# The high and low parts of each streamed weight, issued at the scheduler's highest priority

## The chip, the cores and the metric

The kernel runs on one core of one Trainium2 chip. The metric is device time in microseconds (us), the median of several executions. The core has five engines with one instruction stream each: PE (matrix multiply, with its weight loads listed apart as PEld), DVE (vector), ACT (scalar), POOL and SP, which here only starts DMAs. Each engine runs its own stream strictly in order.

## The reference, cut to what matters

The model has two layers over 256 latent tokens and 256 context tokens, width 1024. Each layer is

```python
h = h + 0.5 * gate * swiglu(modulate(rms_norm(h)), w_up1, w_down1)
u = modulate(rms_norm(h)) @ w_in          # one wide projection
a = [gqa(u), hyena(u), neighbourhood(u), mla(u)]   # four mixers side by side
m = sum_b sigmoid(u_gate[b]) * (a[b] @ w_branch[b])
h = h + gate * (m @ w_out)
h = h + 0.5 * gate * swiglu(modulate(rms_norm(h)), w_up2, w_down2)
```

followed by a last RMS norm of the 256 latent tokens. Everything is float32. All the weights are read once.

## The kernel before, in words

**Three products for one.** A float32 operand x is split into a high part (x rounded to the type fp32r) and a low part (the rest). `split` (L222 to 225) does that with two instructions: a CAST on ACT (L224) writes the high part, a subtraction on DVE (L225) writes the low part and needs the high part first. `mm3` (L246 to 252) then multiplies high by high (L250), high by low (L251) and low by high (L252) into one PSUM bank.

**Weights.** `load` (L227 to 243) brings one block of weights: a tile `raw` in three buffers, filled by one DMA on SP's queue (L235), and the tiles `whi` and `wlo`, most of them in two buffers each. A block of more than 1024 columns is split in two halves, so that each load gives two CASTs and two subtractions. There are 268 loads, 536 halves. In the rows, a CAST of L224 that writes `whi` and a subtraction of L225 that writes `wlo` are these. Other calls of `split` write activations: `ph`/`pl` (feed-forward), `pth`/`ptl` (transposed attention probabilities), `nV`, `gV`, `o`, `mo` and so on; they have the same two lines.

**Stages.** Feed-forward stages stream `up` and `dn` weights through PE. Between them stand a norm (`norm_pair`, output `nh`/`nl`) and the mixers. A mixer works head by head: `head_a` makes the scores `s` (L721), adds a bias in the neighbourhood mixer (L723, from `bm`), takes the negative maximum `nm` (L724), the exponential `P` on ACT (L725), the reciprocal `rs` (L737), and scales `P` on POOL (L740). `head_b` transposes `P` on PE into `ptb` (L755 and L760), splits it into `pth`/`ptl`, and multiplies with the values into `ob` (L767). `of` (L769, L770) collects the heads. In the neighbourhood mixer each head also needs four small DMAs `braw` (L945) on SP's queue, into one buffer, and two POOL additions that make `bm` of it (L948).

**What fills PE beside the heads.** The gates and branch projections (`merge_list`, weights `wmg`, one load a column block: L1085 `th`, L1089, and `merged` on POOL, L1090) are cut in units and dealt out between the heads, so that PE has matmuls `mmb` while a head's chain runs on ACT, DVE and POOL. Layer 0 works on 512 tokens, layer 1 after its first feed-forward on 256, where a matmul is half as wide and there is less to fill with.

**What sets the order.** The kernel is written for a tile framework. It takes the instructions in program order as a rank, lets each engine's next instruction be the one of best rank among those that its model of the chip holds for ready, and writes the five streams out; the streams are then fixed, and on the chip an instruction that waits holds up everything behind it on its engine. `tc.high_priority()` raises whatever is issued inside it above the rest of the kernel.

Of the kernel before, what the change touches and what calls it, by code (L numbers as in the profile page):

```python
# [185 lines left out]
class Net:  # L186
# [40 lines left out]
    def load(self, src, shape, pool=None, bufs=2):  # L227
        nc = self.nc
        n = int(np.prod(shape))
        raw = self.wp.tile([128, 2048], F32, tag="raw", name="raw", bufs=3)  # L230
        hi = (pool or self.wp).tile([128, 2048], F32R, tag="whi", name="whi", bufs=bufs)
        lo = (pool or self.wp).tile([128, 2048], F32R, tag="wlo", name="wlo", bufs=bufs)
        nd = len(shape)
        pat = "p " + " ".join("abcd"[:nd]) + " -> p (" + " ".join("abcd"[:nd]) + ")"
        nc.sync.dma_start(out=raw[:, :n], in_=src.rearrange(pat) if nd > 1 else src)  # L235
        parts = 1 if n <= 1024 else 2
        step = n // parts
        for s in range(0, n, step):
            self.split(hi[:, s:s + step], lo[:, s:s + step], raw[:, s:s + step])
        kw = {"abcd"[i]: shape[i] for i in range(nd)}  # L240
        back = "p (" + " ".join("abcd"[:nd]) + ") -> p " + " ".join("abcd"[:nd])
        if nd == 1:
            return hi[:, :n], lo[:, :n]
        return hi[:, :n].rearrange(back, **kw), lo[:, :n].rearrange(back, **kw)
# [206 lines left out]
    def ffn_lead(self, l, which, n):  # L451
        up = self.a[f"up{which}"][l]

        def lead(load):
            ws = [load(i, up[i], [2, 8, 128]) for i in range(2)]
            ps = [[], []]

            def step(f, k0, a, b):
                if not ps[f]:
                    ps[f] += [self.sbank(), self.bank()] if f else [self.bank(), self.sbank()]  # L460
                for k in range(k0, k0 + 4):
                    for i in range(2):
                        self.mm3(ps[f][i][:, a:b], [(ws[f][0][:, i, k], ws[f][1][:, i, k], self.nh[:, k, a:b], self.nl[:, k, a:b])],
                                 k == 0, k == KT - 1)

            return [lambda f=f, k=k, a=a, b=b: step(f, k, a, b) for g, a, b in self.groups(n) for f in range(2) for k in (0, 4)], ps
        return lead

    def mla_lead(self, l):
        def lead(load):  # L470
            ws = [load(i, self.a["wmkv"][l, i], [4, 288]) for i in range(2)]
            out = []

            def step(g, half):
                if half == 0:
                    out.extend((2 * g + i, (self.sbank() if i else self.bank())[:, 0:288]) for i in range(2))
                wh, wl = ws[half]
                for k in range(4):
                    for tt, p in out[-2:]:
                        s = slice(128 * tt, 128 * tt + 128)  # L480
                        self.mm3(p, [(self.nh[:, 4 * half + k, s], self.nl[:, 4 * half + k, s], wh[:, k, :], wl[:, k, :])],
                                 half == 0 and k == 0, half == 1 and k == 3)

            return [lambda g=g, half=half: step(g, half) for g in range(2) for half in range(2)], out
        return lead
# [826 lines left out]
```

## Time and profile before

| | |
|---|---|
| median of 3 executions | 2529.19 us (2528.36 to 2530.41) |
| profiled execution | 2528.62 us |
| its span | 2526.7 us (1.92 us lie outside it) |
| PE busy | 2444.3 us, 97% of the span |
| DVE, ACT, POOL busy | 1566.2, 1036.5, 322.2 us |
| mean granted TensorE clock | 0.994 of full speed |

A row of the trace names the line, the engine, the operation and the tiles (out <- in, buffer numbers left out). "Idle before" is time in which that engine did nothing ahead of the instruction, with the instruction or DMA that ended it. PE is idle for 82 us in all, which is what an order of instructions could win at most.

### The profile page before, as it was taken

What the parts mean: (1) busy time and instruction counts of PE and PEld (TensorE: products, weight loads), DVE (VectorE), ACT (ScalarE), POOL (GpSimd) and SP (SyncE); (2) the same over time, 40 slices, a digit from 0 to 9 for tenths busy, and PEclk for the clock granted to TensorE, in tenths of its full rate; (3) what the DMA queues carried; (4) which work ended last, traced back from release to release, by engine and by line L of the source; (5) the groups of instructions that cost most, each with busy time, mean ns of one, the idle gap of its engine ahead of it and who ended that gap; (6) DMA issues with size and microseconds to landing.
All of it is one profiled execution on the core that took longest, in us unless ns stands there. A gap on an engine that the chain in (4) does not pass through costs nothing.

```text
span 2526.7 us, 34201 instructions
## 1 busy us (share of the span) xinstructions
PE 2444.3 (97%) x13452; PEld 2089.5 (83%) x13452; DVE 1566.2 (62%) x2520; ACT 1036.5 (41%) x1813; POOL 322.2 (13%) x378
## 2 busy tenths in 40 slices
PE   6999999999989999999999999999999999999998
PEld 3788888877878788788888888888888898798998
DVE  5779865477466555657795355543357767676555
ACT  3422223466236444433222243222246646555443
POOL 3100001111113132211000010000021112221000
PEclk9999999999999999999999999999999999999999
DMA  7556544132212344334563244552232433555453
GB/s 270 209 184 222 202 157 150 57 104 85 95 51 75 72 102 92 121 117 150 184 231 144 84 141 179 174 188 95 76 115 99 143 124 104 104 138 180 153 207 109
DMA packets 80632, 346.74 MB, mean 137 GB/s; under 512 B 24726, under 2 KB 30552, under 8 KB 54360
## 3 DMA queue, kind: packets, MB, share of 16 engines
q1 hardware_dynamic: 78744, 341.41, 40.6%
q10 hardware_dynamic: 1728, 3.15, 0.3%
q8 instruction: 106, 1.74, 0.3%
q14 instruction: 54, 0.44, 0.1%
HBM read 333.52 MB, written 6.82 MB: 135 GB/s over the span
## 4 chain that ended last, share of the span: by engine, by line
PE 77%; issue 10%; DVE 5%; POOL 3%; ACT 3%; DMA 2%; SPq 0%; POOLq 0%; DVEq 0%; ACTq 0%
PE mmb L250 22%; PE mmb L251 22%; PE mmb L252 22%; PE ob L767 2%; PE s L721 1%; DVE wlo L225 1%; DMA braw<-in_rpb 1%; PE ptb L755 1%; POOL P L740 1%; POOL nv L375 1%; ACT whi L224 1%; PE sb L582 1%; PE s L730 1%; PE sb L250 1%; PE sb L252 1%
## 5 line engine op out<-in xcount | busy, mean ns | idle before, releaser
L252 PE MATMUL mmb<-nh,wlo 128*128 128x512 f32 (+1 forms) x2224 | 786.3, 354 | 7.1 <-DVE wlo L225 7.1
L250 PE MATMUL mmb<-nh,whi 128*128 128x512 f32 (+1 forms) x2224 | 787.5, 354 | 3.7 <-ACT nh L374 1.4
L251 PE MATMUL mmb<-nl,whi 128*128 128x512 f32 (+1 forms) x2224 | 785.5, 353 | 3.3 <-DVE nl L376 3.2
L224 ACT CAST whi<-raw 128x1024 fp32r<-128x1024 f32 (+4 forms) x536 | 475.0, 920 | 727.5 <-PE mmb L251 619.6
L225 DVE TENSOR_TENSOR wlo<-raw,whi 128x1024 fp32r<-128x1024 f32 (+4 forms) x536 | 580.8, 1106 | 101.0 <-ACT whi L224 89.0
L252 PEld LDWEIGHTS mmb<-nh,wlo 128*128 128x128 f32 x2224 | 422.0, 190 | 65.0 <-DVE wlo L225 9.5
L251 PEld LDWEIGHTS mmb<-nl,whi 128*128 128x128 f32 x2224 | 422.0, 190 | 61.8 <-DVE nl L376 6.0
L250 PEld LDWEIGHTS mmb<-nh,whi 128*128 128x128 f32 x2224 | 422.5, 190 | 61.1 <-ACT nh L374 2.2
L251 PE MATMUL mmb<-pl,whi 128*128 128x512 f32 (+1 forms) x770 | 267.1, 347 | 0.0
L252 PE MATMUL mmb<-ph,wlo 128*128 128x512 f32 (+1 forms) x770 | 267.1, 347 | 0.0
L250 PE MATMUL mmb<-ph,whi 128*128 128x512 f32 (+1 forms) x770 | 266.8, 347 | 0.0
L430 DVE TENSOR_TENSOR s<-s,mmb 128x512 f32<-128x512 f32 (+1 forms) x85 | 52.7, 620 | 241.1 <-PE mmb L252 233.3
L314 DVE SCALAR_TENSOR_TENSOR vraw<-vraw,cb 128x1024 f32<-128x1024 f32 x128 | 155.5, 1223 | 34.3 <-DMA vraw<-in_adat 27.1
L345 POOL TENSOR_TENSOR rstd<-msq,nhalf 128x2 f32<-128x2 f32 (+1 forms) x11 | 8.4, 765 | 1303.7 <-DVE msq L344 1303.7
L250 PEld LDWEIGHTS mmb<-ph,whi 128*128 128x128 f32 x770 | 145.8, 189 | 18.2
L252 PEld LDWEIGHTS mmb<-ph,wlo 128*128 128x128 f32 x770 | 145.8, 189 | 18.1
L251 PEld LDWEIGHTS mmb<-pl,whi 128*128 128x128 f32 x770 | 145.8, 189 | 17.9
L314 DVE SCALAR_TENSOR_TENSOR scr<-vraw,cb 128x1024 f32<-128x1024 f32 x96 | 117.1, 1220 | 41.3 <-DMA vraw<-in_adat 35.6
L386 DVE SCALAR_TENSOR_TENSOR h<-mmb,mods,h 128x256 f32<-128x256 f32 x136 | 61.2, 479 | 123.9 <-PE mmb L252 123.9
L740 POOL TENSOR_SCALAR P<-P,rs 128x512 f32<-128x512 f32 (+1 forms) x144 | 97.5, 695 | 308.3 <-DVE rs L737 255.3
L429 ACT ACTIVATE s<-mmb 128x512 f32<-128x512 f32 (+1 forms) x85 | 46.4, 546 | 211.2 <-PE mmb L252 211.2
L250 PE MATMUL mmb<-whi,nh 128*128 128x512 f32 (+3 forms) x256 | 89.2, 348 | 2.8 <-ACT nh L374 2.8
(280 smaller groups left out, 3469.0 us busy)
## 6 DMA issues: line engine op xcount, KB each, us to landing
raw<-in_up SPq DMA_DIRECT2D x88, 1024.0 KB, 4.8
vraw<-in_adat SPq DMA_DIRECT2D x64, 1024.0 KB, 4.8
raw<-in_wmg SPq DMA_DIRECT2D x64, 768.0 KB, 4.4
raw<-in_dn SPq DMA_DIRECT2D x64, 704.0 KB, 4.1
raw<-in_wh SPq DMA_DIRECT2D x12, 1024.0 KB, 4.8
araw<-in_adaw SPq DMA_DIRECT2D x8, 1024.0 KB, 9.1
raw<-in_wnqk SPq DMA_DIRECT2D x8, 1024.0 KB, 4.8
raw<-in_wo SPq DMA_DIRECT2D x8, 1024.0 KB, 4.9
```

The lines of the kernel that those rows point to most:

```text
L224: nc.scalar.copy(hi, src)
L225: nc.vector.tensor_tensor(lo, src, hi.bitcast(F32), ALU.subtract)
L250: nc.tensor.matmul(out, wh, xh, start=start and i == 0, stop=False)
L251: nc.tensor.matmul(out, wh, xl, start=False, stop=False)
L252: nc.tensor.matmul(out, wl, xh, start=False, stop=stop and i == n - 1)
L314: nc.vector.scalar_tensor_tensor(out, raw[:, j], 1.0, self.cb[:, s], ALU.mult, ALU.mult, accum_out=mc[:, j, s:s + 1])
L375: nc.gpsimd.tensor_scalar(v[:, i], t[:, i], sc, sh, ALU.mult, ALU.add)
L386: self.nc.vector.scalar_tensor_tensor(h[:, j, a:b], ps[:, a:b], self.mods[l][:, 8 * chunk + j, g:g + 1], h[:, j, a:b], ALU.mult, ALU.add)
L429: nc.scalar.activation(s[:, :n], pa[:, :n], AF.Silu)
L430: nc.vector.tensor_tensor(s[:, :n], s[:, :n], pg[:, :n], ALU.mult)
L740: nc.gpsimd.tensor_scalar(sl, sl, rs[:, qt:qt + 1], 0.0, ALU.mult, ALU.add)
L767: nc.tensor.matmul(ob[:, 0:p.shape[1]], vst(kt), p, start=i + j == 0, stop=i + j == len(pts))
```

## The change

The call of `split` inside `load` is put under `high_priority`. Splits of activations, and those of the Fourier tables that are made elsewhere, keep their rank.

```diff
         for s in range(0, n, step):
-            self.split(hi[:, s:s + step], lo[:, s:s + step], raw[:, s:s + step])
+            with self.tc.high_priority():
+                self.split(hi[:, s:s + step], lo[:, s:s + step], raw[:, s:s + step])
```

No instruction is added or taken away. The same instructions stand in another order: on ACT 146 of the 536 weight CASTs are ahead of something they were behind before (5 are later), on DVE 199 of the subtractions (26 later). The lines below L238 have a number that is one higher in the changed kernel.

**First place: SP's queue in layer 1's neighbourhood mixer.** `raw_18303` is a block of 128x2048 of the query and key weights `wnqk`; `braw` are the bias DMAs of one head each. Before:

```order
L235 DMA raw_18012<-in_wnqk 128x2048
L945 DMA braw_17904<-in_rpb 64x4x64 x4
L235 DMA raw_18115<-in_wmg 128x1536
L945 DMA braw_18088<-in_rpb 64x4x64 x4
L235 DMA raw_18222<-in_wmg 128x1536
L945 DMA braw_18195<-in_rpb 64x4x64 x4
L235 DMA raw_18303<-in_wnqk 128x2048
L235 DMA raw_18406<-in_wmg 128x1536
L945 DMA braw_18379<-in_rpb 64x4x64 x4
```

Now:

```order
L235 DMA raw_18012<-in_wnqk 128x2048
L235 DMA raw_18115<-in_wmg 128x1536
L946 DMA braw_17904<-in_rpb 64x4x64 x4
L235 DMA raw_18222<-in_wmg 128x1536
L946 DMA braw_18088<-in_rpb 64x4x64 x4
L235 DMA raw_18303<-in_wnqk 128x2048
L946 DMA braw_18195<-in_rpb 64x4x64 x4
L235 DMA raw_18406<-in_wmg 128x1536
L235 DMA raw_18513<-in_wmg 128x1536
```

Each weight block has moved ahead of one group of four bias DMAs.

**Second place: ACT in the same stretch.** `pth_18172` and `pth_18181` are the two halves of the transposed probabilities of one head (of `P_17914`, made before these rows), `P_18098` and `P_18205` the exponentials of the next two heads. Before:

```order
L1085 ACTIVATE th_18161<-mmb_18123 128x256
L725 ACTIVATE P_18098,sum_18097<-s_18099,nm_18096 128x512
L725 ACTIVATE P_18098,sum_18097<-s_18105,nm_18096 128x512
L224 CAST whi_18304<-raw_18303 128x1024
L224 CAST pth_18172<-ptb_18167 128x512
L224 CAST pth_18181<-ptb_18176 128x512
L224 CAST whi_18304<-raw_18303 128x1024
L769 COPY of_18165<-ob_18166 64x256
```

Now:

```order
L1086 ACTIVATE th_18161<-mmb_18123 128x256
L224 CAST pth_18172<-ptb_18167 128x512
L726 ACTIVATE P_18098,sum_18097<-s_18099,nm_18096 128x512
L224 CAST whi_18304<-raw_18303 128x1024 x2
L726 ACTIVATE P_18098,sum_18097<-s_18105,nm_18096 128x512
L224 CAST pth_18181<-ptb_18176 128x512
L1086 ACTIVATE th_18268<-mmb_18230 128x256
L770 COPY of_18165<-ob_18166 64x256
```

The first half of `whi_18304` stood ahead of both `pth`; now both of its halves stand behind `pth_18172` and ahead of `pth_18181`.

**Third place: DVE in layer 0's grouped-query mixer (GQA), at a load of `wnv` weights (`wlo_6946`).** `ptl_6663`, `ptl_6672` and `ptl_6681` are the low parts of one head's transposed probabilities. Before:

```order
L1089 SCALAR_TENSOR_TENSOR th_6651<-th_6651,mmb_6614 128x512
L225 TENSOR_TENSOR wlo_6946<-raw_6944,whi_6945 128x1024
L225 TENSOR_TENSOR ptl_6663<-ptb_6657,pth_6662 128x512
L225 TENSOR_TENSOR ptl_6672<-ptb_6666,pth_6671 128x512
L225 TENSOR_TENSOR wlo_6946<-raw_6944,whi_6945 128x1024
L225 TENSOR_TENSOR ptl_6681<-ptb_6675,pth_6680 128x512
```

Now:

```order
L1090 SCALAR_TENSOR_TENSOR th_6651<-th_6651,mmb_6614 128x512
L225 TENSOR_TENSOR wlo_6946<-raw_6944,whi_6945 128x1024 x2
L225 TENSOR_TENSOR ptl_6663<-ptb_6657,pth_6662 128x512
L225 TENSOR_TENSOR ptl_6672<-ptb_6666,pth_6671 128x512
L225 TENSOR_TENSOR ptl_6681<-ptb_6675,pth_6680 128x512
```

The second half of the weight's low part has moved ahead of two low parts of the head. On ACT the second half of `whi_6945` has moved ahead of `pth_6662` and `pth_6671` in the same way.

## Rows read from the trace of the kernel before

**Rows 1.** The page: span, busy time, two groups of instructions.

```profile
span 2526.7 us, 34201 instructions
PE 2444.3 (97%) x13452; PEld 2089.5 (83%) x13452; DVE 1566.2 (62%) x2520; ACT 1036.5 (41%) x1813; POOL 322.2 (13%) x378
...
L224 ACT CAST whi<-raw 128x1024 fp32r<-128x1024 f32 (+4 forms) x536 | 475.0, 920 | 727.5 <-PE mmb L251 619.6
L225 DVE TENSOR_TENSOR wlo<-raw,whi 128x1024 fp32r<-128x1024 f32 (+4 forms) x536 | 580.8, 1106 | 101.0 <-ACT whi L224 89.0
```

**Rows 2.** Busy time by stage (us, instructions); window; last columns clock, DMA share, GB/s.

```profile
100.00:400.00 300.00, 300.00 (x1325) 248.43 (x1324) 235.49 (x394) 82.98 (x111) 0.00 (x0) 1.00 0.54 192
400.00:620.00 220.00, 213.06 (x1166) 181.29 (x1165) 131.65 (x221) 118.20 (x247) 40.41 (x60) 0.99 0.27 85
...
740.00:860.00 120.00, 117.76 (x593) 93.62 (x594) 74.27 (x112) 67.30 (x147) 34.46 (x41) 0.99 0.22 77
...
1925.00:2010.00 85.00, 76.75 (x512) 66.54 (x511) 69.15 (x129) 62.90 (x137) 11.77 (x16) 0.98 0.31 107
...
2140.00:2265.00 125.00, 117.60 (x779) 105.60 (x778) 84.70 (x142) 70.29 (x136) 36.07 (x43) 0.99 0.52 110
```

**Rows 3.** PE's waits over the whole span: us in total, times, longest.

```profile
PE mmb L252 <- DVE wlo L225: 7.1, 6, 3.6
...
PE mmb L250 <- ACT nh L374: 4.2, 3, 1.4
```

**Rows 4.** Timeline of PE, 2204 to 2213 us.

```profile
2204.34 1.04 PE L755 MATMUL ptb<-ident,P 128*128 128x128 f32 x8
2205.14 1.18 PE L721 MATMUL s<-K,Q 128*128 128x512 f32 x4
2211.53 0.58 PE L767 MATMUL ob<-pth,nV 128*128 128x256 f32 x1 [5.21 <-ACT pth L224]
```

**Rows 5.** Timeline of ACT in the same stretch.

```profile
2205.00 0.20 ACT L725 ACTIVATION_READ_ACCUMULATOR P<-s,nm 128x1 f32 x1
2209.94 1.04 ACT L224 CAST whi<-raw 128x1024 fp32r<-128x1024 f32 x1 [4.75 <-DMA raw<-in_wnqk]
2210.89 1.07 ACT L224 CAST pth<-ptb 128x512 fp32r<-128x512 f32 x2
```

**Rows 6.** Timeline of SP's DMA issues, 2168 to 2250 us.

```profile
2184.47 2.57 SPq L945 DMA_DIRECT2D braw<-in_rpb  x4
...
2195.61 2.57 SPq L945 DMA_DIRECT2D braw<-in_rpb  x4
2198.28 0.55 SPq L235 DMA_DIRECT2D raw<-in_wnqk  x1
```

**Rows 7.** Timeline of POOL and DVE, 2184 to 2200 us.

```profile
2185.12 3.69 POOL L740 TENSOR_SCALAR P<-P,rs 128x512 f32<-128x512 f32 x2
...
2195.57 1.36 POOL L740 TENSOR_SCALAR P<-P,rs 128x512 f32<-128x512 f32 x2
...
2187.05 1.20 DVE L225 TENSOR_TENSOR wlo<-raw,whi 128x1024 fp32r<-128x1024 f32 x1
```

**Rows 8.** Timeline of ACT, DVE, PE, POOL, 824 to 831 us.

```profile
825.05 1.05 ACT L224 CAST whi<-raw 128x1024 fp32r<-128x1024 f32 x1 [1.83 <-PE mmb L251]
...
826.12 2.37 DVE L225 TENSOR_TENSOR wlo<-raw,whi 128x1024 fp32r<-128x1024 f32 x1
828.42 1.27 DVE L225 TENSOR_TENSOR ptl<-ptb,pth 128x512 fp32r<-128x512 f32 x2
...
829.15 0.66 PE L755 MATMUL ptb<-ident,P 128*128 128x128 f32 x4 [0.64 <-DVE ptl L225]
...
826.12 1.29 POOL L1090 TENSOR_TENSOR merged<-merged,th 128x512 f32<-128x512 f32 x1 [0.98 <-DVE th L1089]
```

**Rows 9.** Timeline of ACT, 1955 to 1990 us (MLA of layer 1).

```profile
1966.54 0.84 ACT L224 CAST whi<-raw 128x768 fp32r<-128x768 f32 x1 [2.79 <-issue]
...
1969.43 0.84 ACT L224 CAST whi<-raw 128x768 fp32r<-128x768 f32 x1
```

## The prediction, made before the changed kernel ran

> **What bounds the kernel now.** I read the page first: PE is busy for 2444.3 of 2526.7 us [rows 1]. The change makes no instruction shorter, so all it can win lies in the 82.4 us in which PE is idle; what it can lose has no such limit. So the second view is busy time by stage [rows 2]. In the feed-forward stretch from 100 to 400 us PE is busy for 300.00 of 300.00 us: no weight is ever late there, and none can come usefully earlier. The CASTs show why: ACT's idle time before them is 619.6 us for PE, that is, they wait until PE has given back the weight buffer, then run at once, one pair of buffers ahead [rows 1]. PE is idle beside the mixers: 6.9 us from 400 to 620 (MLA of layer 0), 2.2 us from 740 to 860 (GQA of layer 0), 8.3 us from 1925 to 2010 (MLA of layer 1), 7.4 us from 2140 to 2265 (neighbourhood mixer of layer 1) [rows 2].
>
> Third, the list of waits. For a weight's low part, which the change is to bring earlier, PE waits 7.1 us in 6 places, 3.6 us of it in one [rows 3]. The longest of these (at 736 us, behind a normalisation that waits for POOL) and most of the rest have the same neighbours in the new order as in the old, so I count nothing for them. The time that I do count is the other way about: a weight's CAST that holds up an attention head. At 2206.3 us PE has ended the scores `s` and then stands for 5.21 us before `ob` [rows 4], because `pth` is not there. ACT was idle for 4.75 us ahead of a `whi` CAST that waited for its DMA, `raw` of `wnqk`, with `pth` queued right behind it [rows 5].
>
> **The change part by part.**
>
> *No work is added.* 536 CASTs and 536 subtractions (0.920 and 1.106 us each on average [rows 1]) stay what they are. The sum is one of places.
>
> *The neighbourhood mixer of layer 1: −4.6 us.* Two moves bear on the stall. On ACT `pth_18172` now stands ahead of `whi_18304` (second place). Its transposes end at 2205.4 us [rows 4] and the exponentials ahead of it at 2205.2 [rows 5], so it can end near 2206.0, before PE is done with the scores at 2206.3: that wait of 5.21 us goes. The other half, `pth_18181`, stands behind two halves of 1.04 us and an exponential; PE has some 18 matmuls of filling between the two halves in its new order, at 0.12 us about 2.1 us, against 2 x 1.04 + 0.6 = 2.7 us: 0.6 us is left, if the weight has landed. It should have. Before, the DMA was issued at 2198.28 us behind four `braw` that began at 2195.61 [rows 6], and the CAST could start at 2209.94 [rows 5], 11.7 us after the issue. Now it stands ahead of that group, behind the one that began at 2184.47 and took 2.57 us [rows 6]; its buffer comes free when the subtraction that began at 2187.05 ends, at 2188.3 [rows 7]. Issued then, it lands by 2200 even if it takes 11.7 us again, five microseconds before its CAST. So −5.21 + 0.6 = −4.6 us. The bounds: −5.2 if nothing is left, 0 if the wait comes back as another.
>
> *GQA of layer 0: +1.8 us.* Here a weight's second half passes two low parts of a head (third place). Before, the first `wlo` ran from 826.12 for 2.37 us, then two `ptl` for 1.27 together; PE, which needs the `ptl` buffer back before it transposes again, stood for 0.64 us until 829.15 [rows 8]. Now the second `wlo` comes between: 1.20 us [rows 7], so that `ptl_6663` ends near 830.3 instead of 829.1. On ACT `pth_6662` moves back by one CAST, 1.05 us [rows 8]. PE fills some of it: 12 filling matmuls instead of 9 before the next transposes, at 0.227 us each 0.7 us. Net +1.2 − 0.7, about +0.6 us with the rest of the pipeline. There are two such loads (`wnv`). Five or six `wmg` loads among the heads show the same exchange with shorter halves and no stall now; 0.1 us each, together 0.6. Sum 2 x 0.6 + 0.6 = +1.8; bounds 0 (PE finds other filling) and +3.
>
> *MLA of layer 0: +0.5 us.* Weights' halves pass up to ten attention instructions on ACT, and PE takes its filling sooner, so that the late heads have less beside them. PE is idle for 6.9 us in the stretch now [rows 2]. The bounds are 0 and +3, four or five halves of 0.84 us [rows 9] uncovered; as 512-token matmuls still stand between the heads I take a value near the lower end.
>
> *MLA of layer 1: 0.* PE has least to fill with here (8.3 us idle of 85 [rows 2]) and the reorder is largest. At 1966.54 and 1969.43 stand two halves of one load, of 0.84 us each, with five kinds of head work between [rows 9]; now they run next to each other, so that the second half is 2 us earlier and the head work 0.84 us later. PE waited on both sides in this stretch, for weights and for heads. Bounds ±3 us, middle taken.
>
> *Feed-forward and norms: 0.* The halves move ahead of the gated products `s` and their splits. The cover is PE's full queue of ready weights and its second PSUM bank: 24 matmuls of 0.227 us, 5.4 us, against two subtractions of 1.2 us. At the norms they move ahead of a few `nh`; PE's wait there is 4.2 us in all in 3 places [rows 3], and two halves more in front would at worst add half of it, +2 us.
>
> Sum: −4.6 + 1.8 + 0.5 = −2.3 us on the profiled 2528.62, or 2526.3. The median of the runs shown is 0.57 us above the profiled execution, so the forecast is 2526.9 us.
>
> *A rule against the change.* While DVE made weights' low parts, POOL took 3.69 us for two scalings of `P`; ten microseconds later, with no such subtraction beside it, two took 1.36 us [rows 7]. In the other direction the `wlo` of 2.37 us ran beside a POOL addition of 1.29 us [rows 8], twice its 1.20 us. So the two slow each other here by up to 2.3 us. The Trainium skill, page "SBUF — State Buffer", section "SBUF: two separate sides", says that POOL and DVE share one pair of ports as an exclusive lock, also for a DVE operation with two SBUF inputs against a POOL operation that reads SBUF, and that the loser is blocked for the whole instruction. The rows agree with it. What that means for the sum is the third rival below.
>
> **The rivals.**
>
> *The wait only changes its name* (no change, 2529 to 2531 us). The 5.21 us come back as a wait for the next head, since `pth_18181` still stands behind both halves, or for `braw`, which now starts after a 1 MB load. For it: the head's bias DMAs are as slow as the weights. Against it: from 2241 us on heads follow each other on PE at 7 us without a wait. Sum without the gain: +2.3, less a little.
>
> *The weights delay the heads* (slower, 2537 us). In the lean mixers each load now puts its second half, 0.84 to 1.05 us on ACT and 1.2 on DVE, in front of a head's chain. It decides where PE has less than about 2 us of filling between a head's transposes and its `ob`. With 24 heads in the MLA of both layers and GQA of layer 0 at 0.5 us, +12 us, against −4.6: about 2537. For it: ACT and DVE are not the bound anywhere, so the order on them sets only latency, and PE's idle time sits exactly in these stretches. Against it: most heads wait for nothing now, since a head is prepared one ahead.
>
> *The ports* (slower, 2539 us). Two subtractions back to back hold the port for 2.4 us, so POOL's `P` or `merged` is blocked for two instead of one. If half of layer 1's 24 heads lose 1.2 us by it, +14 us − 4.6 = +9.4. It decides where POOL's `P` is the next thing that PE waits for. Against it: the subtractions are as many as before.
>
> *More goes than I count* (faster, 2520 us). In the lean layer 1, earlier loads and earlier low parts remove, beside the 4.6 us, half of the 8.3 us of the MLA stretch and some of the 7.1 us of waits for low parts, without the losses in layer 0: −4.6 − 4.1 = −8.7. For it: three of PE's waits in MLA of layer 1 are for the very operands that move. Against it: it moves heads back in the same place.
>
> **How the numbers follow.** Forecast 0.47 (its own range 2522 to 2531), the wait renamed 0.16, heads delayed 0.13, ports 0.06, more gain 0.18. Something like 0.2%, 5.1 us, is what a measurement can tell from no change, so faster is below 2524.1 and slower above 2534.3. Faster holds the last case and the lower part of the forecast: 0.18 + 0.14 = 0.32. Slower holds the two slower cases and a little of the forecast's upper end: 0.22. The rest, 0.46, is the same. The range must reach from the case of more gain to that of delayed heads: 2518 to 2537.
>
> **What the changed profile would show.** Right: no wait above 1 us for `pth` near 2205 us, `raw` of that `wnqk` issued near 2188 us and not 2198; feed-forward stretches at 100% as before; in GQA of layer 0 PE's waits for `ptl` longer by about half a microsecond at two places; the low-part wait of 3.6 us unchanged. Wrong: a new wait of PE on `P`, `ptl` or `Q` of more than 2 us in a mixer of layer 1 (delayed heads), POOL's `P` rows longer in sum (ports), or PE's idle time from 1925 to 2010 us down by more than 3 us (more gain). The prediction fails outright if the feed-forward stretches are no longer full.

## The result and the profile after

The changed kernel took 2552.45 us (median of 4 executions, 2551.20 to 2554.54) against 2529.78 us before on the same chip: +22.7 us, a ratio of 1.0092 (95% interval 1.0079 to 1.0104). The forecast was 2526.9 us in a range of 2518 to 2537. It was wrong in sign and well outside its range.

The page of the changed kernel: span, busy time, and the groups that answer to [rows 1], with POOL's scaling of `P`.

```profile
span 2552.7 us, 34219 instructions
...
PE 2458.2 (96%) x13452; PEld 2098.6 (82%) x13452; DVE 1569.8 (61%) x2520; ACT 1038.0 (41%) x1813; POOL 324.2 (13%) x378
...
L224 ACT CAST whi<-raw 128x1024 fp32r<-128x1024 f32 (+4 forms) x536 | 466.7, 919 | 727.1 <-PE mmb L252 629.3
L225 DVE TENSOR_TENSOR wlo<-raw,whi 128x1024 fp32r<-128x1024 f32 (+4 forms) x536 | 577.4, 1118 | 106.6 <-ACT whi L224 95.1
...
L741 POOL TENSOR_SCALAR P<-P,rs 128x512 f32<-128x512 f32 (+1 forms) x144 | 95.1, 678 | 317.9 <-DVE rs L738 301.2
```

No engine has more instructions: a CAST takes 0.919 us on average instead of 0.920, a subtraction 1.118 instead of 1.106. PE is idle for 94.5 us instead of 82.4, and its own rows are 13.9 us longer for the same matmuls. The second of these needs an explanation too; the clock gives most of it, in the last section.

Busy time by stage: two stretches of the kernel before (GQA of layer 0 with what leads in, MLA of layer 1), then five of the changed kernel, which are 100 to 400, 700 to 860, 1910 to 2015, 2140 to 2200 and 2200 to 2265 us of the kernel before, moved along with the delay: the feed-forward, the same two, and the neighbourhood mixer of layer 1 in two parts. The third column from the end is the granted clock.

```profile
700.00:860.00 160.00, 154.17 (x807) 125.53 (x806) 97.63 (x172) 81.19 (x174) 41.64 (x45) 0.99 0.18 62
...
1910.00:2015.00 105.00, 94.32 (x619) 81.66 (x618) 82.99 (x157) 71.52 (x155) 13.06 (x17) 0.98 0.35 121
```

```profile
103.00:403.00 300.00, 300.00 (x1325) 248.43 (x1324) 232.78 (x388) 82.32 (x110) 0.00 (x0) 1.00 0.54 191
...
707.00:873.00 166.00, 156.09 (x800) 125.84 (x799) 101.15 (x172) 81.16 (x175) 45.36 (x46) 0.98 0.18 60
...
1930.00:2041.00 111.00, 97.82 (x620) 85.09 (x620) 83.98 (x157) 72.67 (x154) 12.30 (x17) 0.92 0.33 115
2166.00:2226.00 60.00, 59.49 (x360) 51.76 (x359) 40.91 (x66) 34.32 (x64) 14.35 (x18) 1.00 0.51 95
2226.00:2291.00 65.00, 58.94 (x421) 55.22 (x420) 44.79 (x78) 35.57 (x72) 19.24 (x25) 0.95 0.52 124
```

The feed-forward is as full as before. To find where the time went I set PE's matmuls in the order in which they start, in both traces, and took the difference of the k-th start; how much that difference grows while the kernel before passes through a stretch is the stretch's loss. PE has the same number of matmuls in both, and stretches end at the same stages. This is worked out from the profiled executions (2554.54 and 2528.62 us), so its sum is 26.1 us, more than the medians' 22.7. A single stretch scatters: `e9_na1` below, which runs the instructions of the kernel before in the same order up to 2156 us, reads −1.6 in the stretch from 700 to 860 and −0.7 in that to 1910. A figure of this size counts only where several kernels show it.

```
loss in us by stretch (ends in us of the kernel before)
norm ahead of layer 0's mixers     425-470    +3.2
MLA of layer 0                     470-615    -0.1
Hyena of layer 0                   615-700    +2.5
GQA of layer 0 and what leads in   700-860    +6.6
neighbourhood mixer of layer 0     860-1060   +3.4
second feed-forward and its norm  1060-1530   +1.5
feed-forward of layer 1, its norm 1530-1910   +1.7
MLA of layer 1                    1910-2015   +5.8
Hyena and GQA of layer 1          2015-2140   +0.1
neighbourhood mixer of layer 1    2140-2200   -1.3
the same                          2200-2265   +2.0  (-6.4 to 2245, +8.4 after)
the rest, with the first 425 us               +0.8
```

**A head's chain behind a weight, MLA of layer 1.** ACT's timeline in the changed kernel:

```profile
1953.60 1.98 ACT L224 CAST whi<-raw 128x1024 fp32r<-128x1024 f32 x2
1955.60 0.59 ACT L916 ACTIVATE K<-mmb 64x512 fp32r<-64x512 f32 x1
1956.22 0.69 ACT L726 ACTIVATE P<-s,nm 128x512 f32<-128x512 f32 x1
```

and PE's:

```profile
1952.65 0.41 PE L253 MATMUL mmb<-qa,wlo 128*128 128x256 f32 x1
1956.25 1.60 PE L722 MATMUL s<-K,Q 128*128 128x512 f32 x2 [3.19 <-ACT K L916]
```

Both halves of a weight, `whi_15201`, stand in front of the key `K` and the exponential `P` of two heads. PE stands for 3.19 us until `K` is there. It uses the weight first at 1967.89, twelve microseconds after its CASTs. PE's waits in this mixer, first in the kernel before (1910 to 2015 us), then in the changed one (1930 to 2041 us):

```profile
PE mmb L250 <- DVE Q L910: 1.7, 3, 1.4
PE s L721 <- DVE Q L910: 1.2, 1, 1.2
PE mmb L250 <- ACT whi L224: 1.1, 2, 0.9
...
PE mmb L252 <- DVE wlo L225: 0.5, 1, 0.5
```

```profile
PE s L722 <- ACT K L916: 3.6, 2, 3.2
PE s L722 <- DVE Q L911: 2.4, 1, 2.4
PE s L722 <- ACT P L726: 1.2, 1, 1.2
PE mmb L251 <- ACT whi L224: 1.1, 2, 0.9
...
PE mmb L253 <- DVE wlo L225: 0.7, 1, 0.7
```

The waits for weights, 1.6 us, have not shrunk (1.8 now); those of the scores for `K`, `Q` and `P` have grown from 1.2 to 7.2 us.

**The norm ahead of layer 0's mixers.** DVE's timeline, then PE's:

```profile
427.63 0.68 DVE L370 TENSOR_TENSOR nt<-h,ptb 128x512 f32<-128x512 f32 x1
428.23 2.04 DVE L225 TENSOR_TENSOR wlo<-raw,whi 128x768 fp32r<-128x768 f32 x2
430.19 0.68 DVE L377 TENSOR_TENSOR nl<-nv,nh 128x512 fp32r<-128x512 f32 x1
...
438.77 0.58 PE L353 MATMUL ptb<-ones,acc 128*128 128x1 f32 x4 [0.77 <-DVE acc L340]
```

A weight that PE needs at 443.6 us is made in the middle of the norm; in the kernel before the same statistics matmul started at 436.80 without a wait:

```profile
436.80 0.50 PE L352 MATMUL ptb<-ones,acc 128*128 128x1 f32 x4
```

POOL's part of this norm is slower as well, beside those two subtractions. Its six `nv` before, then now:

```profile
425.56 4.25 POOL L375 TENSOR_SCALAR nv<-nt,mods 128x256 f32<-128x256 f32 x6 [1.59 <-DVE nt L369]
...
425.88 5.80 POOL L376 TENSOR_SCALAR nv<-nt,mods 128x256 f32<-128x256 f32 x6 [1.60 <-DVE nt L370]
```

**The start of Hyena in layer 0.** ACT, then PE:

```profile
629.04 1.56 ACT L224 CAST whi<-raw 128x768 fp32r<-128x768 f32 x2 [0.91 <-PE mmb L252]
630.51 1.06 ACT L224 CAST vth<-ptb 128x512 fp32r<-128x512 f32 x2
...
631.14 0.73 PE L251 MATMUL mmb<-vth,dfth 128*128 128x512 f32 x2 [1.04 <-ACT vth L224]
```

**The wait that I wanted to remove, and the one that came.** PE's timeline in the neighbourhood mixer of layer 1, and SP's issues:

```profile
2265.67 0.38 PE L768 MATMUL ob<-ptl,nV 128*128 128x256 f32 x1 [2.39 <-DVE ptl L225]
2271.60 0.47 PE L756 MATMUL ptb<-ident,P 128*128 128x128 f32 x1 [2.44 <-POOL P L741]
...
2208.55 2.58 SPq L946 DMA_DIRECT2D braw<-in_rpb  x4
2211.17 0.60 SPq L235 DMA_DIRECT2D raw<-in_wnqk  x1
2220.39 3.31 SPq L946 DMA_DIRECT2D braw<-in_rpb  x4
...
2257.24 3.50 SPq L946 DMA_DIRECT2D braw<-in_rpb  x4
```

The 5.21 us for `pth` of [rows 4] are gone, and `raw` of `wnqk` is issued at 2211.17, some 12 us earlier than before if the delay of 25 us is taken off. The `braw` groups still follow each other at about 12 us, because their one buffer is free again only when the DMA has landed and POOL has read it. The chain that ended last says the same in the stretch from 2235 to 2272 us:

```profile
2235.49 8.59 DMA braw<-in_rpb
...
2246.93 9.41 DMA braw<-in_rpb
...
2259.20 10.13 DMA braw<-in_rpb
```

### The profile page after: what moved, and what is told of

Its sections match the earlier page's. It is cut to its first block, busy times and chain, and to the rows that moved or that the text cites. A ratio compares the mean times of both kernels' runs of the same rounds, so it can differ in the third digit from the quotient of the medians.

```text
span 2552.7 us, 34219 instructions
## 1 busy us (share of the span) xinstructions
PE 2458.2 (96%) x13452; PEld 2098.6 (82%) x13452; DVE 1569.8 (61%) x2520; ACT 1038.0 (41%) x1813; POOL 324.2 (13%) x378
## 4 chain that ended last, share of the span: by engine, by line
PE 52%; issue 9%; DVE 5%; DMA 3%; POOL 3%; ACT 1%; SPq 1%; POOLq 0%; DVEq 0%; ACTq 0%
PE mmb L252 15%; PE mmb L251 15%; PE mmb L253 15%; DMA braw<-in_rpb 3%; DVE wlo L225 2%; PE s L722 1%; PE ob L768 1%; POOL nv L376 1%; PE ptb L756 1%; SPq L946 1%; ACT whi L224 1%; POOL P L741 0%; POOL grs L346 0%; POOL bm L949 0%; PE sb L252 0%
## 5 line engine op out<-in xcount | busy, mean ns | idle before, releaser
L224 ACT CAST whi<-raw 128x1024 fp32r<-128x1024 f32 (+4 forms) x536 | 466.7, 919 | 727.1 <-PE mmb L252 629.3
L225 DVE TENSOR_TENSOR wlo<-raw,whi 128x1024 fp32r<-128x1024 f32 (+4 forms) x536 | 577.4, 1118 | 106.6 <-ACT whi L224 95.1
L741 POOL TENSOR_SCALAR P<-P,rs 128x512 f32<-128x512 f32 (+1 forms) x144 | 95.1, 678 | 317.9 <-DVE rs L738 301.2
```

Of the source, the lines that this page charges most:

```text
L224: nc.scalar.copy(hi, src)
L225: nc.vector.tensor_tensor(lo, src, hi.bitcast(F32), ALU.subtract)
L741: nc.gpsimd.tensor_scalar(sl, sl, rs[:, qt:qt + 1], 0.0, ALU.mult, ALU.add)
```

## The experiments

Theory A: the raised halves stand in front of a chain (head, norm, transform) on ACT or DVE, and PE waits for the chain. Theory B: it is the bias DMAs behind weight loads on SP. Theory C: DVE and POOL slow each other, as in the prediction's rule against the change. Times are medians against runs of the kernel before on the same chip.

**One engine at a time.** `e1_cast` raises only the CAST, `e2_sub` only the subtraction:

```diff
-            self.split(hi[:, s:s + step], lo[:, s:s + step], raw[:, s:s + step])
+            h_, r_ = hi[:, s:s + step], raw[:, s:s + step]
+            with self.tc.high_priority():
+                nc.scalar.copy(h_, r_)
+            nc.vector.tensor_tensor(lo[:, s:s + step], r_, h_.bitcast(F32), ALU.subtract)
```

(`e1_cast`, against the kernel before; in `e2_sub` the `with` stands around the subtraction instead.)

> Only the CASTs of the weights' high parts are raised, the subtractions keep their rank. SP's order hardly changes (7 weight loads move past other work, against 19). Theory A (the halves stand in front of a head's, a norm's or a transform's chain on ACT and DVE, and PE waits for that chain): part of the loss, +6 to +14 us, with the Hyena start still late because vth stands behind four CASTs. Theory B (the loss is the bias DMAs that now start behind weight loads on SP): at most +3 us. Theory C (DVE and POOL block each other at their shared port): 0, since no DVE instruction is raised.

> Only the subtractions of the weights' low parts are raised. 17 of the 19 weight loads that move on SP still move. Theory A: the other part of the loss, +6 to +14 us. Theory B: nearly all of it, +18 us or more. Theory C: nearly all of it too, with DVE's wlo and POOL's P longer in sum than before (580.8 and 97.5 us).

Measured: `e1_cast` 2542.38 against 2528.42 us, 1.0054 (1.0039 to 1.0069), +14.0 us. `e2_sub` 2533.60, 1.0019 (1.0010 to 1.0029), +5.2 us. So the larger part comes with the raised CASTs, while SP's order hardly moves: at the upper end of A's range for the CASTs, a little under it for the subtractions; B and C fall as explanations of the whole. The two runs do not part ACT from DVE cleanly: a CAST that comes earlier lets its subtraction come earlier, and in `e1_cast` 107 subtractions have moved ahead of other work too. Nor do they add up: 19.2 of 22.7 us, and the neighbourhood mixer of layer 0 loses its 3.4 us only with both (table below). In `e2_sub` the subtractions take 572.8 us in all and POOL's `P` 99.0, against 580.8 [rows 1] and 97.5 before: nothing that would count.

**One kind of load at a time.** `e3_ffn` raises only feed-forward loads, `e4_mix` all others:

```diff
-            with self.tc.high_priority():
+            with self.tc.high_priority() if src.tensor.name[3:5] in ("up", "dn") else ExitStack():
```

> Only the loads of up and dn weights (feed-forward) are raised. Theory A: the feed-forward stretches stay full, and only the norms that overlap with them lose: 0 to +5 us. Theories B and C: 0 (no bias DMA and hardly any POOL work there).

> All loads but up and dn are raised: the complement of the run before. Theory A: +18 to +23 us, and with the feed-forward run together about the whole +23 us. Theories B and C: the whole +23 us.

Measured: `e3_ffn` 2530.44 us, 1.0010 (1.0001 to 1.0020), +2.0 us; `e4_mix` 2549.71 us, 1.0086 (1.0071 to 1.0101), +21.3 us. Together 23.3, the whole of 22.7. In `e3_ffn` the stretch to 1530 us, with its two norms, loses 1.5 us; it loses 1.4 to 1.7 in every kernel that raises both halves of these loads. That to 1910 reads 1.2 without a longer wait, from a longer stay at the lower clock; `e10_mla_exempt`, which raises the same loads, has −0.2 there.

**The bias DMAs.** `e9_na1` raises only the loads in the heads' loop of layer 1's neighbourhood mixer. `e5_after_braw2` and `e6_before_braw2` give the changed kernel and the one before a second buffer for `braw`; `e7_na1_braw2` has both edits:

```diff
-                br = ap.tile([128, 2, 256], F32, tag="braw", name="braw")
+                br = ap.tile([128, 2, 256], F32, tag="braw", name="braw", bufs=2)
```

and in `e9_na1` and `e7_na1_braw2` `self.hot` is true in that loop alone:

```diff
-            with self.tc.high_priority():
+            with self.tc.high_priority() if self.hot else ExitStack():
```

> Only the loads inside the heads' loop of layer 1's neighbourhood mixer are raised. The step of the prediction taken alone: -4.6 us. Theory B1 (this mixer's heads follow the chain of their bias DMAs, one buffer of braw, about 12 us a head, so that PE gets 6 to 7 us ahead and then waits for a later head): -1 to +1 us, with the wait for pth at 2206 us gone and a new one of 5 to 7 us for P or ptl near 2240 to 2255 us.

> The changed kernel with a second buffer for braw, so that a head's bias DMAs needn't wait until the POOL additions have read the one before. Theory B1: the wait that came back at 2263 to 2275 us goes, 5 to 7 us faster than the changed kernel, +16 to +18 us against before. Theory that the heads there wait for the raised halves on ACT and DVE instead: no gain, +22 to +24 us.

> The kernel before with the second buffer for braw alone. Theory B1: here the wait at 2206 us is for a weight, not for a bias, and the bias DMAs now stand even earlier on SP's queue than the weight: -1 to +3 us. If the bias chain bounds this mixer without any help: -4 to -6 us.

> Both together: only the loads in the heads' loop of layer 1's neighbourhood mixer raised, and two buffers for braw. Theory B1: neither wait is left, -5 to -7 us. If the two don't need each other: the sum of the two runs with one of them each.

Measured, against 2529.06 us: `e9_na1` 2529.07, 0.9999 (0.9990 to 1.0009), 0; `e5_after_braw2` 2544.64, 1.0061 (1.0046 to 1.0076), +15.6, just under its range; `e6_before_braw2` 2522.47, 0.9972 (0.9962 to 0.9982), −6.6; `e7_na1_braw2` 2521.82, 0.9970 (0.9959 to 0.9982), −7.2. The step of my prediction taken alone is worth nothing: by the k-th matmul PE is 10.3 us ahead at 2217 us in `e9_na1` (2.8 of them at 2140 us already, where nothing has moved yet), and 8.1 are given back by 2251. PE's waits there, 2140 to 2290 us:

```profile
PE ptb L756 <- POOL P L741: 3.7, 4, 2.4
PE ob L768 <- DVE ptl L225: 2.3, 1, 2.3
```

The surprise is `e6_before_braw2`: I had expected the wait at 2206 us to stay, since it was for a weight. It went, since a weight behind a blocked `braw` on SP waits as well. With the second buffer SP passes on to the weight at 2191.04 instead of 2198.28 [rows 6], and PE's waits in the mixer are down to one row (SP's issues, then PE's waits, 2140 to 2265 us):

```profile
2187.18 3.75 SPq L945 DMA_DIRECT2D braw<-in_rpb  x4
2191.04 0.54 SPq L235 DMA_DIRECT2D raw<-in_wnqk  x1
...
PE ob L767 <- ACT pth L224: 1.1, 3, 0.4
```

So the one buffer of `braw` made the wait before, and with it the one after. `e6_before_braw2` beats both kernels; raising the weights on top of it (`e7_na1_braw2`) adds nothing that can be told. In `e5_after_braw2` the neighbourhood mixer of layer 0 also loses 0.6 us instead of 3.4, so that loss was the bias DMAs' too: theory B holds for these two mixers. (In layer 0 it takes raised gate loads as well: with them exempt, below, the loss is 0.0 with one buffer.)

**Which loads hurt in the mixers.** Three kernels are the changed one with some loads at their old rank: `e8_hyena_exempt` the two gate loads ahead of Hyena in layer 0, `e10_mla_exempt` those of MLA and of Hyena's projections, `e14_gate_exempt` all gate and branch loads (64 of the 274; not 268, since 12 loads are short and give one CAST each); `e15_both_exempt` joins the last two.

```diff
-            with self.tc.high_priority():
+            with ExitStack() if src.tensor.name[3:] == "wmg" else self.tc.high_priority():
...
+            with ExitStack() if src.tensor.name[3:] in ("wmkv", "wmq", "wqr", "wmv", "wqk", "wh") else self.tc.high_priority():
```

> The changed kernel, but the two gate loads that are issued at the start of layer 0's Hyena transform keep their old rank. Theory A: vth and vtl (the transform's input) no longer stand behind four halves on ACT and DVE, PE's waits near 630 us go, and the kernel is 3 to 4.5 us faster than the changed one (+18 to +20 us against before); nothing else moves. If the place is bound by something else: no gain.

> The changed kernel, but the loads of the MLA mixer and of Hyena's projections, both layers (wmkv, wmq, wqr, wmv, wqk, wh), keep their old rank. Theory A: the losses at the norm ahead of layer 0's mixers (3.2 us), in MLA of layer 1 (6 us) and part of that ahead of layer 1's mixers (1.7 us) go: 8 to 11 us faster than the changed kernel, +12 to +15 us against before. If these stretches lose by gate loads that are still raised: at most 3 us faster.

> The changed kernel, but the gate and branch loads (wmg, 64 of the 268) keep their old rank. Theory A: the rest of the mixers' loss is theirs (Hyena start 3 us, heads of GQA and of the neighbourhood mixer in layer 0 some 6 us): 7 to 12 us faster than the changed kernel, +11 to +16 us against before. If the loss there comes from the query, key and value loads: at most 4 us faster.

> The changed kernel, but neither the gate and branch loads nor those of the MLA mixer and Hyena's projections are raised; feed-forward, GQA, neighbourhood and output weights still are. Theory A, with losses that add up: +1 to +5 us against before (the feed-forward's own +2 and two or three heads). If losses move elsewhere when one place is relieved: +8 us or more.

Measured: `e8_hyena_exempt` 2551.69 against 2529.05 us, 1.0089 (1.0074 to 1.0104), +22.6; `e10_mla_exempt` 2542.62, 1.0054 (1.0039 to 1.0069), +13.6; `e14_gate_exempt` 2549.73 against 2528.76, 1.0079 (1.0065 to 1.0093), +21.0; `e15_both_exempt` 2536.16, 1.0028 (1.0017 to 1.0038), +7.4. The losses by stretch, worked out as above from the profiled executions:

```
                 -470  -615  -700  -860 -1060 -1530 -1910 -2015 -2140 -2265
changed           3.2  -0.1   2.5   6.6   3.4   1.5   1.7   5.8   0.1   0.7
e1_cast           0.4  -0.7  -0.3   5.9  -0.2   2.4   0.1   5.9   0.0   0.0
e2_sub            2.4   0.5   1.6  -0.4   0.0   0.5   2.1   0.7  -0.0  -3.9
e8_hyena_exempt   2.4   0.7  -0.5   5.2   4.0   1.7   2.5   6.0   0.0  -0.7
e10_mla_exempt    0.3  -0.7   0.9   5.3   3.8   1.5  -0.2   2.4   0.1  -0.9
e14_gate_exempt   3.2   0.6  -1.3   3.4  -0.0   1.4   2.9   7.3   0.7   2.4
e15_both_exempt   0.3   0.3  -1.3   3.3  -0.0   1.4   0.1   0.0   0.8   2.6
```

`e10_mla_exempt` came where A put it: the norms at 470 and 1910 and more than half of MLA of layer 1 are back. `e8_hyena_exempt` did not show in the median; in its stretch (615 to 700 us) the profiled execution has 3.0 us less, 3.2 less in all, and the interval is as wide as that, so its own verdict is unclear. `e14_gate_exempt` was a miss: 1.7 us saved by the medians where I expected 7 to 12. By stretch the gates do cost what A says (Hyena, GQA and the neighbourhood mixer of layer 0 are 10.4 us better), but 1.2 us come on at the norm at 1910, 1.5 in MLA and 1.7 in the last mixer, and the profiled sum is 4.2 better. Of those 4.4 us 3.2 are time at the lower clock, worked out as in the last section. `e15_both_exempt` is over its range too. MLA of layer 1 loses nothing with both kinds exempt, 2.4 with the gates raised and 7.3 with MLA's own raised, so the parts add up only roughly.

**The height of the raise, and other orders.** `e13_raise40` raises by 40 ranks (`high_priority(offset=40)`). On the kernel with two `braw` buffers, `e12_lower60_braw2` puts the weights 60 ranks later and `e11_chain_braw2` raises `pth`, `ptl`, `vth` and `vtl` instead:

```diff
-            self.split(ph, pl, tb)
+            with self.tc.high_priority():
+                self.split(ph, pl, tb)
```

> All weights' splits are raised by 40 ranks instead of to the front of the whole kernel. Theory A: 40 ranks are a few heads' instructions; fewer chains are passed, so a smaller loss, +3 to +12 us against before. If any raise makes the second half overtake and that alone costs: the whole +20 us or more. If a small raise is what the kernel lacked: faster than before.

> The weights' splits are put 60 ranks later instead of to the front, on the kernel before with two buffers for braw. Theory A: weights have 4 to 8 us in hand in the feed-forward stages and the chains of heads and norms gain: 0 to 4 us faster than without it, -6 to -11 us against before. Rival: the weights become late where PE consumes them fastest and every load loses: slower than before.

> The other way round, on the kernel before with two buffers for braw: the splits of the heads' transposed probabilities (pth, ptl) and of the Hyena input (vth, vtl) are raised, the weights are not. Theory A: a chain that PE waits for is worth raising where it lies behind a weight: 0 to 4 us faster than the same kernel without it, -6 to -11 us against before. If what counts is only that the order was tuned to its ranks and any raise disturbs it: slower than without it by 3 us or more, -3 us or worse.

Measured: `e13_raise40` 2529.59 against 2528.76 us, 1.0001 (0.9992 to 1.0010), +0.8. `e12_lower60_braw2` 2527.98 against 2529.05, 0.9991 (0.9982 to 1.0001), −1.1; `e11_chain_braw2` 2524.25, 0.9981 (0.9972 to 0.9991), −4.8. A raise by 40 ranks costs nothing that can be told, less than I gave it. It also moves less: 21 CASTs are ahead of other work, not 146. So a small raise may be harmless only because it passes few chains; that the distance itself hurts is not shown. Neither other order beats `e6_before_braw2`, where I had expected both to be up to 4 us faster than it. The scatter of `e12_lower60_braw2` is wide (2522.8 to 2529.6 us), and its profiled 2523.48 is at the low end, so that only "no gain" can be said.

## Why the prediction was wrong, point by point

- **Feed-forward 0: right.** 300.00 of 300.00 us, and +2.0 us when only those loads are raised, 1.5 of it in the stretch with two norms.
- **Neighbourhood mixer of layer 1, −4.6 us: the mechanism was right, the gain did not last.** The wait went as described; 0.7 us was lost there in the end. I had named the case, a wait for `braw` in the place of the old one, and set against it that heads follow each other at 7 us without a wait from 2241 us on. That argument failed: the heads could do so, as I read it, because the bias DMAs had caught up during the very wait that the change removes. That the one buffer takes the gain back is shown: `e9_na1` is worth 0 and `e7_na1_braw2` −7.2.
- **MLA of layer 1, 0 within ±3: the step that failed most.** It lost 5.8 us. I took the middle because PE waits on both sides; but a weight that comes early saves at most its own wait, and here that was 1.6 us and stayed, while the head behind it is what PE needs next. `e1_cast` alone gives 5.9, `e15_both_exempt` 0.0. The sign of delayed heads that I had named, a wait of more than 2 us on `P`, `ptl` or `Q` in a mixer of layer 1, came three times: 2.38 on `Q` here, 2.39 on `ptl` and 2.44 on `P` in the neighbourhood mixer.
- **GQA of layer 0, +1.8 within 0 to +3: sign right, mis-sized**, 6.6 us with the normalisation ahead of it. PE's waits for `ptl` came as described, but at more places: 5.0 us in 7 over the whole span, not 1.3 in 2. Half of the loss is the gate loads (3.4 with them exempt), of which I had five or six at 0.1 us each. The low-part wait of 3.6 us [rows 3] stayed, at 4.3.
- **MLA of layer 0, +0.5: right** at −0.1.
- **Norms, 0 to +2: wrong.** 3.2 at the first, some 1.5 each at two others. The price was taken from PE's wait for `nh` of 4.2 us in 3 places [rows 3], that is, from what a short wait costs now, and not from the length of the chain behind which nothing fills PE.
- **Not in the sum at all:** the start of Hyena (2.5 us), the neighbourhood mixer of layer 0 (3.4), and the clock, by which PE's own rows grew by most of 13.9 us in these same stretches.
- **The rivals.** "The weights delay the heads" is what happened, at 22.7 instead of its +8, because norms and a transform are chains too. "The ports" fell where I put them: POOL's `P` takes 95.1 us in all, less than before. But I had looked at the wrong POOL work. At the norm ahead of layer 0's mixers six `nv` take 5.80 us instead of 4.25, beside the subtractions that moved there, and 4.25 again in `e10_mla_exempt`; over the kernel all 88 `nv` take 72.8 us instead of 67.9. How much of the norms' loss is this and how much the order on DVE is not separated.

The misses by stretch (5.3 in the neighbourhood mixer of layer 1, 5.8, 4.8, 6.4 at feed-forward and norms, 2.5 and 3.4) are 28.2 us, nearly all of the 28.4 between the −2.3 forecast and the 26.1 by stretch. What they have in common is that I priced a moved weight by the waits of the kernel before.

Which loads cause the loss is shown for the norms, MLA and the bias DMAs. What is left open is the other half of GQA's 6.6 us (3.3 with both kinds exempt): 3.1 of it lie between 700 and 740 us, ahead of the heads, with a new wait of 1.2 us for `gV`, and GQA's own loads, still raised there, were not exempted. Open is also why `e14_gate_exempt` loses 4.4 us more than the changed kernel in the three later stretches named above. And one rival stands: the new ranks also reorder PE's own stream (in the changed kernel another row stands at 2109 of its 13452 places), so that filling can be used up early. No run holds PE's order fixed, so how much of a head's wait is its own delay and how much the missing filling is not known.

## What to carry to other kernels

A raised priority is paid by whoever stands behind it in an in-order queue. Before raising a producer, look at who waits: here the weights had microseconds in hand and the chains none, so the front of the queue was the wrong end, and a raise by 40 ranks, which moved little, was as good as none. When a wait for one thing goes, ask what ran on during it: the buffer with the longest cycle (here 12 us for one `braw` buffer) takes its place, and a second buffer there was worth more than any order that was tried, −6.6 us.

## What the runs showed of the hardware that was not expected

A stop of PE can be followed by a slower PE. Busy time by window in the changed kernel, around the 3.19 us wait in MLA of layer 1 (it ends at 1956.25, and a wait of 2.4 us for `Q` had ended at 1948.94); third from the end is the granted clock:

```profile
1944.00:1950.00 6.00, 3.62 (x20) 2.73 (x20) 5.29 (x9) 4.98 (x10) 0.00 (x0) 1.00 0.30 78
1950.00:1953.00 3.00, 3.00 (x14) 2.59 (x12) 2.88 (x6) 2.34 (x5) 0.00 (x0) 0.57 0.72 303
1953.00:1957.00 4.00, 0.81 (x2) 0.29 (x1) 2.44 (x3) 3.95 (x8) 0.00 (x0) 0.50 0.00 0
1957.00:1960.00 3.00, 2.99 (x8) 2.10 (x8) 2.81 (x8) 2.13 (x8) 1.37 (x2) 0.50 0.36 109
1960.00:1963.00 3.00, 3.00 (x25) 3.00 (x25) 2.62 (x6) 2.13 (x5) 0.31 (x1) 0.89 0.00 0
```

After six microseconds in which PE was busy for 3.62 the clock falls to 0.50, which is 1.2 of 2.4 GHz, before the 3.19 us wait begins, and stays there across it and three microseconds beyond. A score matmul of 128x512 then takes 0.63 us in its row, where those of this mixer took 0.39 to 0.50 before the change. The busy time times what the clock lacks is 3.00 x 0.43 + 0.81 x 0.50 + 2.99 x 0.50 + 3.00 x 0.11 = 3.5 us, beside two waits of 5.6 us together. The kernel before passed this place at a clock of 1.00, though PE had waits here too:

```profile
1930.00:1933.00 3.00, 1.60 (x12) 1.25 (x12) 2.88 (x5) 2.94 (x7) 0.00 (x0) 1.00 0.45 104
...
2206.00:2211.00 5.00, 0.32 (x2) 0.00 (x0) 0.84 (x2) 1.06 (x2) 2.75 (x4) 1.00 0.70 249
2211.00:2214.00 3.00, 2.47 (x11) 2.48 (x12) 2.23 (x4) 1.91 (x3) 0.00 (x0) 0.57 0.56 39
2214.00:2217.00 3.00, 3.00 (x24) 3.00 (x23) 1.28 (x3) 1.38 (x4) 0.74 (x1) 0.86 0.80 126
```

The last three are its 5.21 us wait, which cost 2.47 x 0.43 + 3.00 x 0.14 = 1.5 us more by the clock. So the price of a wait differs from place to place, and no fixed factor comes out of these rows. Over the whole profiled executions the same product is 23.4 us in the changed kernel and 11.1 before (4.8 of the difference in MLA of layer 1): 12.3 of the 13.9 us by which PE's own rows grew for the same matmuls. None of my terms had it, since they counted waits alone; nor were the 82.4 us of idle time all that an order could win, with 11.1 us more in the clock. The Trainium skill, page "TensorE: Matmul & The Clock Gate", section "Part 1: The HAM clock gate (the "warmup" mystery)", says that the clock passes half or all of its pulses by how busy PE has been; these rows show both levels.
